# Where the split of the values' weights stands in layer 0 of a two-layer transformer kernel, and which engine makes its low parts

## The chip, the cores and the metric

The kernel runs on one core of one Trainium2 chip. The metric is the device time of one execution in microseconds (us). A core has five engines with instruction queues of their own: PE (TensorE, matrix products), DVE (VectorE), ACT (ScalarE), POOL (GpSimd) and SP (SyncE, which here only issues DMAs). Each engine works through its queue in the order in which it was built; engines wait for each other by semaphores.

## The reference

Two layers of a parallel-branch trunk are computed on 512 latent tokens and 256 context tokens of width 1024, in float32. Cut to what matters:

```python
hx = _rmsnorm(x, norm_g) * (1.0 + scale_x) + shift_x      # adaLN: scale and shift from c @ w_ada
px = hx @ w_in                                            # one projection, 5376 columns
a_k, a_v, b_k, b_v, a_q, b_q, a_z, b_z, g_a, g_b = _split(px, SPLIT_SIZES)
a_att = _na_latent(qa, ka, va, cka, cva, rpb, rows)       # neighbourhood attention, ka = rmsnorm(a_k)
b_att = _gqa_latent(qb, k_all, v_all)                     # grouped-query attention
out_x = _merge(a_att, b_att, a_z, b_z, g_a, g_b, w_o_a, w_o_b, w_out)
x_new = x + gate_x * out_x
```

The context tokens go through the same weights (in layer 0 all of them, in layer 1 only keys and values). The change concerns the first microseconds of layer 0: the norm and modulation of `x`, the first projection (`a_k`, the keys) and the second one (`a_v`, the values).

## The kernel before, in words

**Products in three parts.** A float32 operand is split into a high part (a cast to `fp32r`, made on ACT) and a low part (the difference of operand and high part, made on DVE or POOL). A product is then three matmuls (`mm3`, lines 351 to 353): high x high, high x low and low x high, all into one PSUM tile.

**Weights.** `load_w` (line 313) brings eight blocks of 128 x 512 of a weight matrix: a DMA on SP into a tile `raw` (three buffers in all), the cast `whi<-raw` on ACT (line 321), the low part `wlo<-raw,whi` (line 324) on the engine that `lo_eng(k)` names. `mix_lo` names VectorE for odd blocks and GpSimd for even ones. A `raw` buffer is free for the next DMA when its low part has been made. `whi` and `wlo` have eight buffers each, which the first projection's weights hold before the values' weights do.

**The start.** The first projection of layer 0 (the keys: six token tiles of 128, eight weight blocks, 144 matmuls) is woven into loads, norms, transposes and the adaLN modulation by `start_run` (line 1053). Its order is the string `START`, a list of tokens. The tokens that matter here carry the number of a channel block (0 to 7): `wh`/`wl` make the two parts of a weight block, `dot7.v` are four dot products on VectorE (line 1117, `jk<-wx,rawy`) that yield the modulation of block 7, `mf` turns sums into the two modulation columns (lines 208 and 209), `ts` applies them (line 1140 on ACT, 1142 on VectorE), `hi` and `lo` make the parts of the modulated activations (lines 1132 and 1134, `hx<-yT`), and `Pt.k` is token tile t times weight block k: three matmuls. After all tokens, `in_program_order` (line 392) ties each engine's instructions of the start to each other in the order of the string.

**What follows it.** `layer` (line 490) then evacuates the six PSUM tiles of the keys (copy to `y`, squares on ACT, sums on VectorE, the inverse root on POOL, lines 285 and 287), and calls `load_w` for the values' weights (line 620) and `tok_proj` for six token tiles (line 624): 24 matmuls each. The first of them writes PSUM tile `psf_818`, the second `psx_851`. Next come the weights of the queries (line 628). Everything outside the start is placed by the framework's scheduler: it works with a model of time and puts an instruction into an engine's queue where it expects it to be ready, if no tie forbids that. Nothing tied the eight casts and low parts of line 620 to the start, so that the scheduler was free to put them between the start's own instructions.

Of the kernel before, what the change touches and what calls it, by code (L numbers as in the profile page):

```python
# [22 lines left out]
KT = DM // 128  # L23
# [10 lines left out]
ON_PE, ON_DVE, ON_SP = mybir.EngineType.PE, mybir.EngineType.DVE, mybir.EngineType.SP  # L34
ON_ACT, ON_POOL = mybir.EngineType.Activation, mybir.EngineType.Pool
# [19 lines left out]
C_AK, C_AV, C_BKV, C_AQ, C_BQ, C_AZ, C_BZ, C_GA, C_GB = (  # L55
    0, 512, 1024, 1280, 1792, 2304, 2816, 3328, 4352)
# [6 lines left out]
def F(ap):  # L63
    return ap.bitcast(F32)
# [3 lines left out]
def hybrid_kernel(es: ExitStack, tc, x, ctx, cvec, w_ada, w_ada0, small, gvec, w_in, w_o_a, w_o_b, w_out,  # L68
                  bias_int, bias_edge, rope, ident_d, out):
    nc = tc.nc  # L70
    V, S, G, T = nc.vector, nc.scalar, nc.gpsimd, nc.tensor
# [10 lines left out]
    def nm(s):  # L82
        uid[0] += 1
        return f"{s}_{uid[0]}"

    def big(name):
        return bigp.tile([128, 3072], F32, tag="big", name=nm(name))
# [106 lines left out]
    def raw_tile():  # L194
        return wp.tile([128, 512], F32, tag="raw", name=nm("raw"), bufs=3)
# [117 lines left out]
    def load_w(src, col0, n, nk, lo_eng, k0=0, own=None, bufs=8):  # L313

        pool, x = (wp, "") if own is None else (own, "x")
        res = []
        for k in range(k0, k0 + nk):
            raw = raw_tile()
            nc.sync.dma_start(raw[:, :n], src[128 * k:128 * k + 128, col0:col0 + n])
            hi = pool.tile([128, 512], F32R, tag="whi" + x, name=nm("whi"), bufs=bufs)  # L320
            S.copy(hi[:, :n], raw[:, :n])  # L321
            lo = pool.tile([128, 512], F32R, tag="wlo" + x, name=nm("wlo"), bufs=bufs)
            e = lo_eng(k)
            e.tensor_tensor(lo[:, :n], raw[:, :n], F(hi[:, :n]), ALU.subtract)  # L324
            res.append((hi, lo))
        return res

    def load_w2(src, col0, nk, lo_eng):

        res = []  # L330
        for i in range(nk // 2):
            raw = raw_tile()
            nc.sync.dma_start(raw.rearrange("p (k n) -> p k n", k=2),
                              src[256 * i:256 * i + 256, col0:col0 + 256].rearrange("(k p) n -> p k n", k=2))
            hi = wp.tile([128, 512], F32R, tag="whi", name=nm("whi"), bufs=8)
            S.copy(hi, raw)  # L336
            lo = wp.tile([128, 512], F32R, tag="wlo", name=nm("wlo"), bufs=8)
            lo_eng(i).tensor_tensor(lo, raw, F(hi), ALU.subtract)  # L338
            res += [(hi[:, c:c + 256], lo[:, c:c + 256]) for c in (0, 256)]
        return res  # L340
# [3 lines left out]
    mix_lo = lambda k: V if k % 2 == 1 else G  # L344
# [44 lines left out]
                    mybir.DependencyClass.NoSync, mybir.DependencyReason.DATA), reason="program order")  # L389
                last = i.name  # L390

    def in_program_order(engines, seq):

        last = {}
        for i in seq:
            if i.engine in engines:
                if i.engine in last:
                    tc.add_manual_dep(i, last[i.engine], mybir.DependencyInfo(
                        mybir.DependencyClass.NoSync, mybir.DependencyReason.DATA), reason="program order")
                last[i.engine] = i.name  # L400

    def turn_late(n):

        while len(hp["late"]) > n:
            behind(ON_PE, hp["late"].pop(0))
# [84 lines left out]
    def layer(l, hx, nxt, mid):  # L490
        first = l == 0
# [4 lines left out]
        W = w_in[l]  # L496
# [114 lines left out]
        else:  # L611
            hp["p"] = bgp_es.enter_context(tc.tile_pool(name=f"cp{l}", bufs=1, reuse_waits="tile"))
            w = load_w(W, C_AK, 512, KT, mix_lo)
# [3 lines left out]
            run(bg, 1)  # L617
        per_bg = -(-len(bg) // (2 + qt))
        va = [big("va0"), big("va1")]
        w = load_w(W, C_AV, 512, KT, mix_lo)  # L620
        for t in range(6):
            if first:
                hp["lag"] = max(4 - t, 0)
# [4 lines left out]
        w = load_w(W, C_AQ, 512, KT, mix_lo, own=hp["p"])  # L628
# [18 lines left out]
        if True:  # L647
# [262 lines left out]
            w = load_w2(W, C_BKV, KT, mix_lo)  # L910
# [81 lines left out]
        with tc.tile_pool(name=f"mrg{l}", bufs=1, reuse_waits="tile") as mp:  # L992
# [37 lines left out]
            for n in range(2):  # L1030
                w = load_w(w_out[l], 512 * n, 512, KT, mix_lo)
# [21 lines left out]
    def start_run(wk, mm):  # L1053
# [91 lines left out]
        done, at = nc.cur_bb.bb.instructions, len(nc.cur_bb.bb.instructions)  # L1145
        for i in range(WARM):
            T.transpose(start_ps[5][:, 0:128], ident, ident)
        seq = list(done[at:])
        for tok in START.split():
            at = len(done)  # L1150
            if tok in setup:
                seq += done[setup[tok]]
            else:
                step(tok)
                seq += done[at:]
        in_program_order((ON_PE, ON_SP, ON_DVE, ON_ACT, ON_POOL), seq)

    start_w, start_ps, hx1 = {}, [], []

    def nxt():  # L1160
        if not hx1:
            hx1.extend([[big("hx") for _ in range(2)] for _ in range(2)])
        return hx1
    layer(0, hx0, nxt, start_run)
    layer(1, hx1, None, None)


# [69 lines left out]
```

## Time and profile before

| | |
|---|---|
| time, median of 3 runs | 1154.84 us (1154.14 to 1155.36) |
| the profiled execution | 1154.87 us |
| its span | 1152.3 us |
| mean granted TensorE clock | 0.998 |
| DMA | 135.08 MB, mean 117 GB/s |

The span runs from the first instruction to the last; 2.57 us of the execution lie around it. In the profile, rows of the timeline give the start in us from the span's start, the busy time in us, engine, line, operation and tiles; "x2" at a row's end means two instructions that were merged into it, and what stands in brackets is idle time before it with what ended it. PE rows are matmuls, which overlap: what counts is the distance from start to start. SPq rows are DMA issues.

### The profile page before, as it was taken

Reading aid. Unit: us, or ns where it says so; the run is one execution under the profiler, and the core shown is the slowest. Engines: PE = TensorE matmul, PEld = TensorE weight load, DVE = VectorE, ACT = ScalarE, POOL = GpSimd, SP = SyncE. Lnnn points to the kernel's source line nnn. Section 1 sums busy time; section 2 is a strip of 40 time slices with the busy share of each in tenths; the row PEclk is TensorE's granted clock in tenths of the full one; section 3 lists DMA queues with packets and bytes.
Section 4 is the critical chain, followed back from the end, with each engine's and each line's share of the span. In section 5 each row is a group of like instructions: output and inputs, shape, how many; then the busy total and the mean of one; then the engine's idle time right before and its main releaser. Section 6 shows DMA issues by size and latency. Waiting matters only on the chain.

```text
span 1152.3 us, 17437 instructions
## 1 busy us (share of the span) xinstructions
PE 1125.1 (98%) x6136; PEld 950.1 (82%) x6136; DVE 821.1 (71%) x1529; ACT 579.4 (50%) x1185; POOL 487.9 (42%) x453
## 2 busy tenths in 40 slices
PE   7899999999999999999999999999999999999998
PEld 5688888989988888878788787888888988887786
DVE  6866688997464687698588755569787665898563
ACT  6553266665433465566330365346666445766521
POOL 1172354454365243354411127245563664465321
PEclk9999999999999999999999999999999999999999
DMA  9734222233332332460343523533332333152133
GB/s 368 237 121 138 73 81 65 84 112 98 107 128 71 100 101 74 75 269 23 128 161 101 173 74 110 183 98 116 105 106 83 111 101 101 65 174 92 64 128 92
DMA packets 89694, 135.08 MB, mean 117 GB/s; under 512 B 10788, under 2 KB 52744, under 8 KB 88968
## 3 DMA queue, kind: packets, MB, share of 16 engines
q1 hardware_dynamic: 89328, 133.87, 36.6%
q8 instruction: 48, 0.79, 0.3%
q14 instruction: 38, 0.31, 0.1%
q10 hardware_dynamic: 280, 0.12, 0.0%
HBM read 116.63 MB, written 17.32 MB: 116 GB/s over the span
## 4 chain that ended last, share of the span: by engine, by line
PE 78%; DVE 8%; DMA 6%; issue 3%; ACT 3%; POOL 2%; SPq 0%; ACTq 0%; POOLq 0%; DVEq 0%
PE psx L353 12%; PE psx L351 11%; PE psx L352 11%; PE psf L351 9%; PE psf L353 9%; PE psf L352 9%; PE pst L666 4%; PE pss L715 2%; PE pss L716 2%; DMA raw<-in_w_in_dram 2%; PE psv L970 2%; PE pss L792 1%; PE pst L431 1%; PE psv L969 1%; DVE ptl L670 1%
## 5 line engine op out<-in xcount | busy, mean ns | idle before, releaser
L670 DVE TENSOR_TENSOR ptl<-pst,pth 128x512 fp32r<-128x512 f32 (+1 forms) x176 | 116.0, 672 | 46.7 <-ACT pth L669 45.6
L669 ACT CAST pth<-pst 128x512 fp32r<-128x512 f32 (+1 forms) x176 | 99.3, 577 | 87.3 <-PE pst L666 56.4
L338 POOL TENSOR_TENSOR wlo<-raw,whi 128x512 fp32r<-128x512 f32 x68 | 94.6, 1394 | 107.8 <-ACT whi L336 86.6
L351 PE MATMUL psx<-whi,hx 128*128 128x512 f32 (+1 forms) x368 | 138.3, 377 | 1.5 <-ACT hx L1132 1.5
L351 PE MATMUL psf<-hx,whi 128*128 128x512 f32 (+1 forms) x368 | 139.2, 378 | 0.0
L353 PE MATMUL psx<-whi,hx 128*128 128x512 f32 (+1 forms) x368 | 136.4, 371 | 2.1 <-DVE hx L1134 2.1
L352 PE MATMUL psf<-hx,whi 128*128 128x512 f32 (+1 forms) x368 | 138.1, 375 | 0.0
L353 PE MATMUL psf<-hx,wlo 128*128 128x512 f32 (+1 forms) x368 | 137.8, 374 | 0.0
L352 PE MATMUL psx<-wlo,hx 128*128 128x512 f32 (+1 forms) x368 | 135.9, 369 | 0.0
L324 POOL TENSOR_TENSOR wlo<-raw,whi 128x512 fp32r<-128x512 f32 x40 | 58.7, 1468 | 141.5 <-ACT whi L321 106.1
L336 ACT CAST whi<-raw 128x512 fp32r<-128x512 f32 x136 | 82.5, 622 | 50.8 <-DMA raw<-in_w_in_dram 32.5
L321 ACT CAST whi<-raw 128x512 fp32r<-128x512 f32 x88 | 54.0, 623 | 105.6 <-PE psx L353 41.8
L666 PE MATMUL pst<-ident,p 128*128 128x128 f32 x640 | 99.9, 272 | 1.4 <-DVE ptl L670 0.8
L666 PEld LDWEIGHTS pst<-ident,p 128*128 128x128 f32 x640 | 77.8, 140 | 13.0 <-DVE ptl L670 1.3
L338 DVE TENSOR_TENSOR wlo<-raw,whi 128x512 fp32r<-128x512 f32 x68 | 69.3, 1020 | 26.1 <-ACT whi L336 25.5
L655 POOL TENSOR_SCALAR r<-r 128x1 f32<-128x1 f32 x64 | 22.3, 349 | 151.7 <-DVE r L650 144.7
L656 POOL TENSOR_TENSOR p<-p,r 128x512 f32<-128x512 f32 (+1 forms) x64 | 83.9, 1310 | 5.1
L353 PEld LDWEIGHTS psx<-whi,hx 128*128 128x128 f32 x368 | 69.7, 189 | 14.6 <-DVE hx L1134 2.8
L351 PEld LDWEIGHTS psx<-whi,hx 128*128 128x128 f32 x368 | 69.7, 190 | 14.2 <-ACT hx L1132 2.3
L353 PEld LDWEIGHTS psf<-hx,wlo 128*128 128x128 f32 x368 | 69.4, 189 | 11.8
L352 PEld LDWEIGHTS psx<-wlo,hx 128*128 128x128 f32 x368 | 69.7, 189 | 10.8
L351 PEld LDWEIGHTS psf<-hx,whi 128*128 128x128 f32 x368 | 69.4, 188 | 10.8 <-ACT zt L516 0.2
(252 smaller groups left out, 3056.3 us busy)
## 6 DMA issues: line engine op xcount, KB each, us to landing
raw<-in_w_in_dram SPq DMA_DIRECT2D x168, 256.0 KB, 2.9
rawb<-in_w_ada_dram SPq DMA_DIRECT2D x64, 256.0 KB, 2.9
gs<-zt SPq DMA_DIRECT2D x32, 256.0 KB, 2.1
raw<-in_w_out_dram SPq DMA_DIRECT2D x32, 256.0 KB, 3.0
tg<-gs SPq DMA_DIRECT2D x4, 1536.0 KB, 7.4
rawx<-in_w_ada_dram SPq DMA_DIRECT2D x8, 512.0 KB, 7.7
raw<-in_w_o_a_dram SPq DMA_DIRECT2D x16, 256.0 KB, 2.7
raw<-in_w_o_b_dram SPq DMA_DIRECT2D x16, 256.0 KB, 2.8
```

The costliest lines, as they stand in the source:

```text
L321: S.copy(hi[:, :n], raw[:, :n])
L324: e.tensor_tensor(lo[:, :n], raw[:, :n], F(hi[:, :n]), ALU.subtract)
L336: S.copy(hi, raw)
L338: lo_eng(i).tensor_tensor(lo, raw, F(hi), ALU.subtract)
L351: T.matmul(ps, lhs[0], rhs[0], start=first, stop=False)
L352: T.matmul(ps, lhs[0], rhs[1], start=False, stop=False)
L353: T.matmul(ps, lhs[1], rhs[0], start=False, stop=last)
L656: G.tensor_tensor(p[:, c0:c1], p[:, c0:c1], r[:, i:i + 1].to_broadcast([128, c1 - c0]), ALU.mult)
L666: T.transpose(pt[:, c0:c0 + 128], src, ident)
L669: S.copy(hi[:, n0:n1], pt[:, n0:n1])
L670: V.tensor_tensor(lo[:, n0:n1], pt[:, n0:n1], F(hi[:, n0:n1]), ALU.subtract)
L715: T.matmul(ps[:, c0:c0 + n], q, sl(kh), start=True, stop=False)
```

## The change

The casts and low parts of the values' weights in layer 0 get a tie: in the program's order, their instructions on VectorE and ScalarE follow the last instruction that the start has on that engine. For that, `in_program_order` takes and returns the table of each engine's last instruction, and the start leaves it in `start_last`. The DMAs of these weights are not tied. Also, in layer 0 all eight low parts of these weights are made on VectorE, where blocks 0, 2, 4 and 6 were made on GpSimd. Layer 1 keeps `mix_lo` and has no tie. All else in the program's text stays; as the scheduler places what is not tied, the order of other instructions can follow.

```diff
-    def in_program_order(engines, seq):
+    def in_program_order(engines, seq, last):
 
-        last = {}
         for i in seq:
             if i.engine in engines:
                 if i.engine in last:
                     tc.add_manual_dep(i, last[i.engine], mybir.DependencyInfo(
                         mybir.DependencyClass.NoSync, mybir.DependencyReason.DATA), reason="program order")
                 last[i.engine] = i.name
+        return last
...
-        w = load_w(W, C_AV, 512, KT, mix_lo)
+        at = len(nc.cur_bb.bb.instructions)
+        w = load_w(W, C_AV, 512, KT, (lambda k: V) if first else mix_lo)
+        if first:
+            in_program_order((ON_DVE, ON_ACT), nc.cur_bb.bb.instructions[at:], start_last)
...
-        in_program_order((ON_PE, ON_SP, ON_DVE, ON_ACT, ON_POOL), seq)
+        start_last.update(in_program_order((ON_PE, ON_SP, ON_DVE, ON_ACT, ON_POOL), seq, {}))
 
-    start_w, start_ps, hx1 = {}, [], []
+    start_w, start_ps, start_last, hx1 = {}, [], {}, []
```

The order of the built program shows two places of it. The first is VectorE at the end of the start, from the reduction of `mf6` (line 1121; 1124 in the changed kernel, whose lines below the edit stand three further down) to the first evacuation of the keys. `wlo` rows of line 324 are low parts of the values' weights, rows that write `jk` are the dot products, and `hx_102` is the low part of the activations. Before:

```order
L1121 TENSOR_REDUCE sums_613<-pst_604 128x4
L324 TENSOR_TENSOR wlo_780<-raw_776,whi_778 128x512
L208 TENSOR_SCALAR modc<-sums_613,bsc,g_128 128x2
L209 TENSOR_SCALAR modc<-sums_613,gcol 128x2
...
L324 TENSOR_TENSOR wlo_792<-raw_788,whi_790 128x512
L1134 TENSOR_TENSOR hx_102<-yT_104,hx_100 128x768
L208 TENSOR_SCALAR modc<-sums_594,bsc,g_128 128x2
L209 TENSOR_SCALAR modc<-sums_594,gcol 128x2
L324 TENSOR_TENSOR wlo_804<-raw_800,whi_802 128x512
L1134 TENSOR_TENSOR hx_102<-yT_104,hx_100 128x768
L453 COPY y_707<-psx_135 128x512
```

And the same place on VectorE in the changed kernel:

```order
L1124 TENSOR_REDUCE sums_613<-pst_604 128x4
L208 TENSOR_SCALAR modc<-sums_613,bsc,g_128 128x2
L209 TENSOR_SCALAR modc<-sums_613,gcol 128x2
...
L1137 TENSOR_TENSOR hx_102<-yT_104,hx_100 128x768
L208 TENSOR_SCALAR modc<-sums_594,bsc,g_128 128x2
L209 TENSOR_SCALAR modc<-sums_594,gcol 128x2
L1137 TENSOR_TENSOR hx_102<-yT_104,hx_100 128x768
L324 TENSOR_TENSOR wlo_774<-raw_770,whi_772 128x512
L324 TENSOR_TENSOR wlo_780<-raw_776,whi_778 128x512
L324 TENSOR_TENSOR wlo_786<-raw_782,whi_784 128x512
L453 COPY y_707<-psx_135 128x512
```

Three low parts (of blocks 1, 3 and 5) stood between the start's instructions and now stand behind its last one, with those of blocks 0 and 2 from GpSimd's queue.

The second place is TensorE where the values' projection begins, behind the last three matmuls of the keys (`psx_138`). `whi_772`, `whi_778`, `whi_784` and `whi_790` are blocks 0 to 3. From the changed kernel:

```order
L353 MATMUL psx_138<-whi_570,hx_102 128x512
L351 MATMUL psf_818<-whi_772,hx_99 128x512
...
L353 MATMUL psf_818<-whi_784,hx_101 128x512
L351 MATMUL psf_818<-whi_790,hx_99 128x512
L351 MATMUL psx_851<-whi_772,hx_99 128x512
L352 MATMUL psx_851<-wlo_774,hx_99 128x512
L353 MATMUL psx_851<-whi_772,hx_101 128x512
L351 MATMUL psx_851<-whi_778,hx_99 128x512
L352 MATMUL psx_851<-wlo_780,hx_99 128x512
L353 MATMUL psx_851<-whi_778,hx_101 128x512
L352 MATMUL psf_818<-wlo_792,hx_99 128x512
```

Before, the first token tile went through seven blocks before the second one began; now six matmuls of the second tile stand between the first and the second matmul of block 3, because the scheduler expects block 3's low part later than before. TensorE's queue up to the end of the keys is the same in both.

## The prediction

> **What bounds the kernel now.** The page's engine line comes first:
>
> ```profile
> PE 1125.1 (98%) x6136; PEld 950.1 (82%) x6136; DVE 821.1 (71%) x1529; ACT 579.4 (50%) x1185; POOL 487.9 (42%) x453
> ```
>
> TensorE is busy for 98% of the span: time is won only where it stands or runs slowly. So the next view is who TensorE waited for:
>
> ```profile
> PE psx L353 <- DVE hx L1134: 2.1, 1, 2.1
> PE psv L970 <- DVE ptl L670: 2.0, 3, 1.5
> PE psx L351 <- ACT hx L1132: 1.5, 1, 1.5
> ```
>
> Behind the first load, the longest single waits are for `hx`, the activations' parts that the start makes. The table by stage (span, then busy time of PE, PEld, DVE, ACT, POOL, then granted clock) shows what stands around them:
>
> ```profile
> 45.00:49.50 4.50, 4.50 (x22) 3.65 (x20) 4.50 (x7) 0.62 (x2) 3.34 (x2) 1.00 0.38 117
> 49.50:51.33 1.83, 0.33 (x3) 0.00 (x1) 1.83 (x5) 1.39 (x3) 0.00 (x0) 1.00 0.51 143
> 51.33:55.40 4.07, 1.99 (x7) 1.34 (x8) 3.09 (x6) 1.41 (x3) 1.40 (x1) 1.00 0.39 103
> 55.40:58.78 3.38, 3.38 (x10) 2.60 (x9) 1.65 (x2) 1.60 (x3) 0.00 (x0) 0.51 0.89 288
> 58.78:62.00 3.22, 3.22 (x15) 2.66 (x14) 0.22 (x1) 1.60 (x3) 0.41 (x1) 0.99 0.36 138
> 1000.00:1100.00 100.00, 96.97 (x502) 78.45 (x501) 82.69 (x124) 61.84 (x116) 48.31 (x42) 1.00 0.30 101
> ```
>
> From 49.50 to 55.40 TensorE stands for over half the time, VectorE is nearly always busy, and then for 3.38 us the clock is 0.51. TensorE's own rows there:
>
> ```profile
> 46.04 0.39 PE L353 MATMUL psx<-whi,hx 128*128 128x512 f32 x1
> ...
> 49.44 0.39 PE L353 MATMUL psx<-whi,hx 128*128 128x512 f32 x1
> 51.33 0.50 PE L351 MATMUL psx<-whi,hx 128*128 128x512 f32 x1 [1.50 <-ACT hx L1132]
> 51.66 0.40 PE L352 MATMUL psx<-wlo,hx 128*128 128x512 f32 x1
> 54.14 0.50 PE L353 MATMUL psx<-whi,hx 128*128 128x512 f32 x1 [2.08 <-DVE hx L1134]
> ...
> 58.78 0.43 PE L351 MATMUL psx<-whi,hx 128*128 128x512 f32 x1
> ...
> 64.30 0.39 PE L351 MATMUL psf<-whi,hx 128*128 128x512 f32 x1
> ```
>
> From 46.04 to 49.44 lie 15 distances: 0.227 us per matmul undisturbed; I use 0.228. The row at 51.33 is the first matmul of `P5.6`, which needs `hi6`; the row at 54.14 its third, which needs `lo6`; 58.78 is `P5.7`; 64.30 is the first matmul of the values.
>
> What held `hx` back is on VectorE, and beside it on POOL:
>
> ```profile
> 37.35 0.17 DVE L1121 TENSOR_REDUCE sums<-pst 128x4 f32<-128x16 f32 x1 [0.18 <-PE pst L1110]
> 37.56 0.29 DVE L208 TENSOR_SCALAR modc<-sums,bsc,g 128x2 f32<-128x2 f32 x1
> 37.76 0.22 DVE L209 TENSOR_SCALAR modc<-sums,gcol 128x2 f32<-128x2 f32 x1
> ...
> 45.42 0.17 DVE L1121 TENSOR_REDUCE sums<-pst 128x4 f32<-128x16 f32 x1
> 45.50 1.69 DVE L324 TENSOR_TENSOR wlo<-raw,whi 128x512 fp32r<-128x512 f32 x1
> 47.11 1.25 DVE L208 TENSOR_SCALAR modc<-sums,bsc,g 128x2 f32<-128x2 f32 x1
> 48.27 0.22 DVE L209 TENSOR_SCALAR modc<-sums,gcol 128x2 f32<-128x2 f32 x1
> 48.41 1.21 DVE L1117 CUSTOM_DVE_ANT_0 jk<-wx,rawy 128x1024 bf16<-128x1024 f32 x1
> ...
> 49.55 0.86 DVE L1142 TENSOR_SCALAR yT<-yT,modc 128x512 f32<-128x512 f32 x2
> 50.33 1.21 DVE L1117 CUSTOM_DVE_ANT_0 jk<-wx,rawy 128x1024 bf16<-128x1024 f32 x1
> ...
> 51.47 0.68 DVE L324 TENSOR_TENSOR wlo<-raw,whi 128x512 fp32r<-128x512 f32 x1
> 52.08 2.01 DVE L1134 TENSOR_TENSOR hx<-yT,hx 128x768 fp32r<-128x768 f32 x1
> 54.01 0.28 DVE L208 TENSOR_SCALAR modc<-sums,bsc,g 128x2 f32<-128x2 f32 x1
> 54.20 0.22 DVE L209 TENSOR_SCALAR modc<-sums,gcol 128x2 f32<-128x2 f32 x1
> ...
> 57.04 0.96 DVE L1134 TENSOR_TENSOR hx<-yT,hx 128x768 fp32r<-128x768 f32 x1
> ```
>
> ```profile
> 44.31 4.03 POOL L324 TENSOR_TENSOR wlo<-raw,whi 128x512 fp32r<-128x512 f32 x2 [20.32 <-ACT whi L321]
> 51.87 1.40 POOL L324 TENSOR_TENSOR wlo<-raw,whi 128x512 fp32r<-128x512 f32 x1 [3.54 <-ACT whi L321]
> ```
>
> Two low parts of the values' weights stand in front of `mf6` and of `lo6`. Beside POOL's low parts VectorE's instructions stretch: line 324 takes 1.69 instead of 0.68 us, line 208 1.25 instead of 0.29, `lo6` 2.01 instead of the 0.96 of `lo7`.
>
> **The change part by part: the start.** Without rows of line 324 on VectorE, and with POOL's gone from there, I set VectorE's rows together anew from 45.42, with undisturbed distances: 0.21 to line 208, 0.20 to line 209, 0.13 (48.27 to 48.41 is 0.14) to the dot product at 45.96, 1.14 to `ts6` at 47.10, 0.78 to the last dot product at 47.88, 1.14 to `lo6` at 49.02, done at 49.98. For `hi6` and `ts7` ACT's rows give the lengths:
>
> ```profile
> 50.44 0.83 ACT L1132 CAST hx<-yT 128x768 fp32r<-128x768 f32 x1 [0.44 <-DVE yT L1142]
> ...
> 54.46 1.31 ACT L1140 ACTIVATE yT<-yT,modc 128x512 f32<-128x512 f32 x2 [2.66 <-DVE modc L209]
> 55.67 0.60 ACT L321 CAST whi<-raw 128x512 fp32r<-128x512 f32 x1
> 56.18 0.83 ACT L1132 CAST hx<-yT 128x768 fp32r<-128x768 f32 x1
> ```
>
> `ts6` ends at 47.96, `hi6` at 48.82. TensorE would reach `P5.6` at 49.44 + 0.228 = 49.67 and needs `lo6` two matmuls later, at 50.12: the first wait goes, the second goes with some 0.1 us to spare (54.09 to 54.14: 0.05 pass between the end of `lo6` and its reader). A row of VectorE begins 0.08 before the last one ends (54.01 against 54.09), so `mf7` begins at 49.90 and ends, as at 54.01 to 54.42, at 50.3; `ts7` runs from 50.36, `hi7` starts 1.21 later and ends at 52.40, `lo7` at 53.38. `P5.7` stands 15 matmuls behind `P5.6`, at 53.09, and needs `lo7` at 53.55: again 0.1 us to spare. What is late next is therefore this same chain; I allow 0.1 us for it, and 0.6 as its bad end (0.3 at each of the two places).
>
> From 49.44 to 64.30 are 14.86 us and 40 distances (39 matmuls of 13 groups, and the first of the values); 40 x 0.228 = 9.12. The difference, **5.74 us**, is what the start can win, and it has three parts: 1.66 (51.33 less 49.67), 2.25 (54.14 less 51.89), and the rest, 1.83, at the 0.51 clock and the first matmuls behind a wait. The clock part alone is 3.38 x 0.49 = 1.66, by the stage row.
>
> That this last part goes with the waits is an inference. For it: the slow stretch begins 1.3 us behind the second wait, and of the stages above only the one behind two long waits is slow. Against it: the 1.5 us wait of line 970 lies between 1000 and 1100, where the clock stayed at 1.00. [...] I follow the rows, a low clock right behind the only place with two long waits within 5 us, and keep the other as a rival.
>
> **The values' weights.** They are what the change puts at risk. ACT casts blocks 0 to 2 behind `hi7`, at 0.6 us each from 52.4 to 54.3; VectorE makes their low parts behind `lo7`, at 0.68 us each, done at 54.1, 54.7 and 55.4. The values now begin at 58.56 instead of 64.30: blocks 0 to 2 are ready 3 us before. Blocks 3 to 7 wait for a `raw` buffer, so each DMA starts only when the low part three blocks earlier is done. The answer for line 319 gives the flight:
>
> ```profile
> DMA to landing us min/median/max: 2.6/2.7/9.8
> ```
>
> Block 3: issued 54.1, landed 56.8, cast 57.4, low part 58.1. TensorE wants its cast behind nine matmuls, at 60.6, and its low part behind six more, at 62.2: 3.2 and 4.1 us to spare. Block 6 is next on that buffer: issued 58.1, landed 60.8, cast by 61.6 and low part by 62.9, as each stands behind one or two evacuations of the keys (an estimate: 0.6 to 0.7 us apiece). Its cast is wanted behind 30 matmuls and four transposes, at 65.8. No wait. On VectorE four low parts more are 4 x 0.68 = 2.7 us, in a place where it was idle for 3.0 of 3.22 us (row 58.78 to 62.00); TensorE wants the keys' evacuations only in the transposes between the values' matmuls, the first of them 30 matmuls in, at 65.4. POOL loses four low parts and is free sooner for its inverse roots. On SP the two loads of `cb` and two of `rawb` for later dot products now stand before block 3's; they wait only for matmuls from before 30 us, land in the ten us before block 3's is due, and cost nothing; were they late by a flight, it would be 2.7 of the 3.2 us to spare.
>
> **Later.** Between 60 and 150 us TensorE shows no wait; queues from there to the merge of layer 0 are the same, so the shift passes on whole. In the merge and layer 1 a few instructions swap places. I take 0, and 1 us either way as bounds.
>
> Sum: 1154.87 - 5.74 + 0.1 = **1149.2 us** (its span 1146.7). The profiled execution lies 0.03 from the median, so it stands for it. Own range: 1148.2 (nothing lost, 0.9 won later) to 1150.2.
>
> **The rivals.** A measurement of this kernel can tell 0.2%, 2.3 us, from no change.
>
> *The slow clock stays* (10%): 1149.2 + 1.66 = 1150.9. For it: the gaps are short and one of 1.5 us elsewhere had no such effect. Against: of the other stages above, none with TensorE busy throughout is slow.
>
> *Given back later* (13%): the swapped instructions, or evacuations that now meet the values' matmuls sooner, bring 1 to 3.3 us of new waits: 1150.2 to 1152.5. For it: TensorE's listed waits for `ptl`, up to 1.5, depend on close races. Against: the order of almost all queues is kept.
>
> *The values' weights come late: slower* (4%). If flights took L instead of 2.7, block 6, which hangs on two flights in a row, would be late from 2 x (L - 2.7) = 4.2, L = 4.8. At L = 7 block 3's wait (1.1) and its own (3.1) come to 4.2 us, and with a second slow clock (1.66) eat 5.74: that is where it turns slower. At the longest flight seen, 9.8, the waits are 3.9 and 5.9, so 1149.2 + 9.8 + 1.7 = 1160.7. Against: 2.7 is the median, and the 9.8 lies in the start's dense loads.
>
> *No effect* (3%): 1154.9, if something else that I don't see paces `hx`. The order of VectorE speaks against it.
>
> The forecast keeps 70%. The range 1148.0 to 1151.3 holds it, the slow clock, and a third of "given back": 84%. Faster by over 2.3 us: 70 + 10 + 12 = 92%, of which I keep 0.9; same 0.06; slower 0.04.
>
> **What would show it.** Right: no wait of TensorE for `hx` over 0.3 us between 45 and 60, clock 1.00 there, the first values' matmul near 58.6, line 324 at about 0.68 on VectorE, `lo6` near 0.96. Wrong: a wait for `whi` or `wlo` at line 351 or 352 between 58 and 70 (the weights), a clock near 0.5 after 50 (the rival's 1.66), or a first values' matmul near 58.6 with a span that shrank by less than 4.5 (given back).

## The result and the profile after

The changed kernel took 1148.99 us (median of 4 runs, 1148.41 to 1149.14), the kernel before in the same job 1155.1 us (4 runs, 1154.14 to 1156.52): the ratio is 0.9945, 95% interval 0.9928 to 0.9962. The profiled execution of after took 1149.07 us.

The page of after opens with its span and the engines' busy time:

```profile
span 1147.0 us, 17434 instructions
...
PE 1123.5 (98%) x6136; PEld 949.2 (83%) x6136; DVE 818.3 (71%) x1533; ACT 580.3 (51%) x1185; POOL 483.0 (42%) x449
```

The span is 5.3 us shorter; another 0.5 us is missing around it (2.07 us instead of 2.57). Asked who TensorE waited for between 20 and 150 us, the trace of after lists nobody; before it listed the two waits for `hx`. The stages (span, busy time of PE, PEld, DVE, ACT, POOL, then granted clock), in the stretches that the prediction used:

```profile
49.50:51.33 1.83, 1.83 (x9) 1.42 (x8) 0.88 (x3) 0.91 (x2) 0.00 (x0) 1.00 0.00 0
51.33:55.40 4.07, 4.07 (x19) 3.15 (x18) 2.77 (x4) 3.33 (x6) 0.00 (x0) 1.00 0.06 7
55.40:58.78 3.38, 3.38 (x17) 2.79 (x16) 2.50 (x4) 2.55 (x6) 1.09 (x2) 1.00 0.69 229
```

TensorE is busy through all three, and where 0.51 stood the clock is 1.00. VectorE in the timeline of after, from the reduction of `mf6` on:

```profile
45.50 0.17 DVE L1124 TENSOR_REDUCE sums<-pst 128x4 f32<-128x16 f32 x1
45.71 0.29 DVE L208 TENSOR_SCALAR modc<-sums,bsc,g 128x2 f32<-128x2 f32 x1
...
47.96 1.22 DVE L1120 CUSTOM_DVE_ANT_0 jk<-wx,rawy 128x1024 bf16<-128x1024 f32 x1
...
49.10 0.95 DVE L1137 TENSOR_TENSOR hx<-yT,hx 128x768 fp32r<-128x768 f32 x1
49.97 0.28 DVE L208 TENSOR_SCALAR modc<-sums,bsc,g 128x2 f32<-128x2 f32 x1
50.16 0.22 DVE L209 TENSOR_SCALAR modc<-sums,gcol 128x2 f32<-128x2 f32 x1
52.62 0.96 DVE L1137 TENSOR_TENSOR hx<-yT,hx 128x768 fp32r<-128x768 f32 x1 [2.24 <-ACT hx L1135]
53.50 1.89 DVE L324 TENSOR_TENSOR wlo<-raw,whi 128x512 fp32r<-128x512 f32 x3
```

`lo6` (49.10) starts 3.60 us behind the reduction, not 6.66; it takes 0.95 instead of 2.01 us, line 208 behind the reduction 0.29 instead of 1.25. The three low parts come behind `lo7` (52.62), in 1.89 us together. TensorE's rows, `P5.6` with its third matmul, `P5.7` with its third and the one behind it, and the first of the values:

```profile
49.74 0.39 PE L351 MATMUL psx<-whi,hx 128*128 128x512 f32 x1
...
50.19 0.41 PE L353 MATMUL psx<-whi,hx 128*128 128x512 f32 x1
...
53.19 0.39 PE L351 MATMUL psx<-whi,hx 128*128 128x512 f32 x1
...
53.64 0.50 PE L353 MATMUL psx<-whi,hx 128*128 128x512 f32 x1
53.97 0.39 PE L351 MATMUL psf<-whi,hx 128*128 128x512 f32 x1
...
58.76 0.39 PE L351 MATMUL psf<-whi,hx 128*128 128x512 f32 x1
```

The values start 5.54 us sooner (64.30 to 58.76). From there to the end of the span are 1088.24 us, before 1088.0: 0.24 us is given back. The one wait of TensorE that is new in the later part lies between 900 and 1000 us; a wait of 0.4 for `whi`, between 500 and 800 us, is gone:

```profile
PE psf L351 <- ACT zt L516: 0.6, 1, 0.6
```

### The profile page after: what moved, and what is told of

Same layout as the page of the kernel before. It is cut to its first block, busy times and chain, and to the rows that moved or that the text cites. A ratio compares the mean times of both kernels' runs of the same rounds, so it can differ in the third digit from the quotient of the medians.

```text
span 1147.0 us, 17434 instructions
## 1 busy us (share of the span) xinstructions
PE 1123.5 (98%) x6136; PEld 949.2 (83%) x6136; DVE 818.3 (71%) x1533; ACT 580.3 (51%) x1185; POOL 483.0 (42%) x449
## 4 chain that ended last, share of the span: by engine, by line
PE 80%; DVE 7%; DMA 4%; issue 3%; ACT 3%; POOL 2%; SPq 0%; POOLq 0%; ACTq 0%; DVEq 0%
PE psx L353 12%; PE psx L352 12%; PE psx L351 11%; PE psf L351 9%; PE psf L352 9%; PE psf L353 9%; PE pst L669 4%; DMA raw<-in_w_in_dram 2%; PE pss L718 2%; PE pss L719 2%; PE psv L973 2%; PE psv L972 1%; PE pss L795 1%; PE pst L431 1%; DMA rawb<-in_w_ada_dram 1%
## 5 line engine op out<-in xcount | busy, mean ns | idle before, releaser
L338 POOL TENSOR_TENSOR wlo<-raw,whi 128x512 fp32r<-128x512 f32 x68 | 95.6, 1409 | 105.1 <-ACT whi L336 83.9
L324 POOL TENSOR_TENSOR wlo<-raw,whi 128x512 fp32r<-128x512 f32 x36 | 50.9, 1416 | 110.0 <-ACT whi L321 74.6
```

## The experiments

The theory: low parts of line 324 ahead of the start's instructions on VectorE, and GpSimd's beside them, held `hx` back; the two waits that followed also lowered the clock. The rivals: only one half of the edit matters; the slow stretch has another cause; the weights are close to being late. One measure runs through what follows. It is the distance from the third matmul of `P5.6`, the reader of `lo6`, to the first matmul of the values: 37 distances of the same work in every kernel, all behind the waits at `P5.6`.

### The tie alone

The change, with the low parts shared out as before:

```diff
-        w = load_w(W, C_AV, 512, KT, (lambda k: V) if first else mix_lo)
+        w = load_w(W, C_AV, 512, KT, mix_lo)
```

> The tie alone: low parts of blocks 0, 2, 4, 6 stay on GpSimd. Theory (what stood ahead of lo6 and lo7 in VectorE's queue, and GpSimd beside it, made the waits): nearly all of the gain stays, 1149.3 to 1150.0 us; the 0.3 to 1.0 us lost against the change is lo7, which now runs beside GpSimd's first low part (0.96 stretched towards 2.0), seen as a wait of TensorE for hx near 53.6. Rival (the choice of VectorE brings half of the gain): about 1152, with TensorE waiting for wlo from GpSimd behind 58 us.

Measured: 1149.09 us (5 runs, 1148.67 to 1149.74), ratio to before 0.9953 (0.9941 to 0.9964): the change's own time within the spread of either. The loss that was expected at `lo7` did not come. VectorE and then GpSimd there:

```profile
52.73 0.96 DVE L1137 TENSOR_TENSOR hx<-yT,hx 128x768 fp32r<-128x768 f32 x1 [2.24 <-ACT hx L1135]
53.77 1.61 DVE L324 TENSOR_TENSOR wlo<-raw,whi 128x512 fp32r<-128x512 f32 x1
```

```profile
53.30 3.24 POOL L324 TENSOR_TENSOR wlo<-raw,whi 128x512 fp32r<-128x512 f32 x2 [29.48 <-ACT whi L321]
```

`lo7` had started when GpSimd's low part began at 53.30, and kept 0.96 us; the next instruction of VectorE, at 53.77, took 1.61 instead of 0.68. So the stretch is there again, in a place where nobody waits for it. The tie does the work.

### The engine alone

The kernel before, with all eight low parts on VectorE and no tie:

```diff
-        w = load_w(W, C_AV, 512, KT, mix_lo)
+        w = load_w(W, C_AV, 512, KT, (lambda k: V) if first else mix_lo)
```

> VectorE alone, without the tie. The scheduler now puts five low parts ahead of lo6 on VectorE (two ahead of mf6, one ahead of ts6, two ahead of lo6). Theory: GpSimd's stretch goes (3.0 us on VectorE's rows before), queueing grows from two to five low parts (3 x 0.61 us more). Set together from 45.5: hi6 ends at about 51.1, lo6 at 52.9, two waits of TensorE of 1.5 and 1.3 us; the values' first matmul at 61.4 with the clock at 1.00, at 63.1 with a slow stretch. Time 1152.0 to 1153.7. Rival (only the place in the queue counts, GpSimd's neighbourhood nothing): three more low parts, slower than before, about 1157.

Measured: 1153.75 us (11 runs, 1152.17 to 1154.53), ratio 0.999 (0.9981 to 0.9998). TensorE's waits between 20 and 150 us, then VectorE:

```profile
PE psx L351 <- ACT hx L1132: 1.4, 1, 1.4
PE psx L353 <- DVE hx L1134: 0.9, 1, 0.9
PE pst L431 <- DVE y L419: 0.6, 1, 0.6
```

```profile
45.70 1.28 DVE L324 TENSOR_TENSOR wlo<-raw,whi 128x512 fp32r<-128x512 f32 x2
46.91 0.28 DVE L208 TENSOR_SCALAR modc<-sums,bsc,g 128x2 f32<-128x2 f32 x1
...
52.10 0.95 DVE L1134 TENSOR_TENSOR hx<-yT,hx 128x768 fp32r<-128x768 f32 x1
```

Without GpSimd beside it none of these rows stretches: 0.28 instead of 1.25, 0.95 instead of 2.01, a low part 0.64. But five low parts stand ahead of `lo6`, so the wait for `hi6` stays and the second one falls only to 0.9. So the stretching beside GpSimd accounts for part of the waits (2.08 against 0.93 us for `lo6`); moving it away without the tie puts three more low parts in the same way, and wins 0.1%.

### The tie on VectorE only, and the low parts on GpSimd

Two more versions of the tie. In the first, ScalarE's casts are free again, and those of blocks 0 to 2 go back ahead of `hi6`; in the second, `pool_lo` names GpSimd for every block:

```diff
-            in_program_order((ON_DVE, ON_ACT), nc.cur_bb.bb.instructions[at:], start_last)
+            in_program_order((ON_DVE,), nc.cur_bb.bb.instructions[at:], start_last)
```

```diff
-        w = load_w(W, C_AV, 512, KT, (lambda k: V) if first else mix_lo)
+        w = load_w(W, C_AV, 512, KT, pool_lo if first else mix_lo)
```

> The change with the tie on VectorE alone: the casts of blocks 0 to 2 may stand ahead of hi6 on ScalarE again, the low parts may not. Theory (the low parts made the waits, the casts none, since ScalarE had 0.4 us and more of idle time ahead of hi6): as the change, 1148.5 to 1149.5. Rival (the casts ahead of hi6 hold it back, 0.62 us each): up to 0.6 us more wait at P5.6, about 1149.6 to 1150.2.

> The tie, with all eight low parts of the values' weights on GpSimd. Theory (the weights had 3 to 4 us to spare, and the order on TensorE follows what the scheduler expects): lo7 stretched as with the tie alone, 0.3 to 1.0 us, and 0 to 2 us of waits for wlo behind 58 us: 1149.3 to 1152. Rival (the weights are close to late as soon as they are tied): waits for wlo of 4 us and more, 1153 or over, with a slow clock behind them.

Measured: 1148.47 us (5 runs, 1148.36 to 1149.92; ratio 0.9947, 0.9934 to 0.9961) and 1148.92 us (5 runs, 1148.46 to 1149.37; ratio 0.9947, 0.9935 to 0.996). Both stand with the change, the second below the 1149.3 that was the least expected. In the first, the last two of ScalarE's casts of blocks 0 to 2 stand from 43.85 to 45.10, 2.49 us of idle time ahead of `hi6`. So they cost nothing there, and with the low parts behind the start their engine made no difference in the time (1148.99 us on VectorE, 1149.09 shared out, 1148.92 on GpSimd). Even GpSimd, at 4.05 us for three of them, is early enough; its row, and beside it `lo7` on VectorE, which again began first and kept 0.96:

```profile
52.81 4.05 POOL L324 TENSOR_TENSOR wlo<-raw,whi 128x512 fp32r<-128x512 f32 x3 [28.98 <-ACT whi L321]
```

```profile
52.24 0.96 DVE L1137 TENSOR_TENSOR hx<-yT,hx 128x768 fp32r<-128x768 f32 x1 [2.24 <-ACT hx L1135]
```

### Every block loaded twice

The change, with the DMA of each of the eight blocks issued twice in a row into the same buffer (`times` is 2 for the values' weights of layer 0 and 1 elsewhere):

```diff
-            nc.sync.dma_start(raw[:, :n], src[128 * k:128 * k + 128, col0:col0 + n])
+            for _ in range(times):
+                nc.sync.dma_start(raw[:, :n], src[128 * k:128 * k + 128, col0:col0 + n])
```

> The change with each block of the values' weights loaded twice into the same buffer, one DMA after the other, which makes the flight about 5.4 instead of 2.7 us. By the prediction's working (block 3 to spare 3.2 us, block 6 behind two flights late from 4.8): block 6 late by 2 x 2.7 - 4.2 = 1.2 us if TensorE's order were kept; the scheduler mixes three token tiles now, which hides more. Theory: 0 to 1.2 us more than the change, 1149.0 to 1150.2. Rival (weights near their limit): 3 us more or worse, 1152 and over.

Measured: 1149.48 us (5 runs, 1148.67 to 1150.72), ratio 0.9954 (0.9941 to 0.9966), and again no wait of TensorE from 20 to 110 us. The casts of the blocks on ScalarE (line 322 there), the row at 60.20 being block 3:

```profile
51.60 1.66 ACT L322 CAST whi<-raw 128x512 fp32r<-128x512 f32 x3
60.20 0.62 ACT L322 CAST whi<-raw 128x512 fp32r<-128x512 f32 x1 [1.81 <-DMA raw<-in_w_in_dram]
61.73 0.61 ACT L322 CAST whi<-raw 128x512 fp32r<-128x512 f32 x1
62.78 0.61 ACT L322 CAST whi<-raw 128x512 fp32r<-128x512 f32 x1
```

Block 3's cast starts 3.4 us later than in after (56.80), and nobody waited for it: the scheduler, which knows of the second load, put other matmuls first (the first one of block 3 starts at 63.29, in after at 60.80). In a kernel placed for it, then, even a doubled flight is not late. The change's own order on TensorE is not tested by it: nine matmuls behind this run's first of the values (58.30), that order would want the cast at 60.34, and it ends at 60.82, so an estimate is 0.5 us late.

### The waits filled with transposes

The kernel before, with 12 transposes of the identity ahead of `P5.6` (the token `F0.12`) and 16 between its second and third matmul, into a PSUM tile that nobody reads. `hx` comes as late as before, but TensorE has something to do meanwhile:

```diff
         T.matmul(ps, lhs[0], rhs[0], start=first, stop=False)
         T.matmul(ps, lhs[0], rhs[1], start=False, stop=False)
+        if fz is not None:
+            for i in range(16):
+                T.transpose(fz, ident, ident)
         T.matmul(ps, lhs[1], rhs[0], start=False, stop=last)
```

> The kernel before with its two waits for hx, but 12 transposes of the identity matrix into a spare PSUM tile in TensorE's queue ahead of P5.6 and 16 between its second and third matmul, so that TensorE works while it would wait (about 1.3 of 1.7 and 1.8 of 2.2 us). Theory (the slow clock comes from TensorE's idleness in the waits): the waits stay as long, the clock stays at 1.00, the slow stretch of 3.38 us goes: 1.5 to 1.7 us less than before, about 1153.4. Rival (the slow stretch has another cause): clock 0.51 stays behind 55, time as before, 1155.

Measured: 1154.65 us (12 runs, 1153.43 to 1158.99), ratio 1.0005 (0.9995 to 1.0016): in the time, nothing; some 1.5 us had been expected. In the profile, the stage and TensorE's rows at `P5.6` (line 356 is the third matmul of each product there):

```profile
55.40:58.78 3.38, 3.38 (x16) 2.62 (x15) 1.46 (x2) 2.38 (x4) 0.00 (x0) 1.00 0.89 259
```

```profile
52.55 1.91 PE L355 MATMUL pst<-ident 128*128 128x128 f32 x16
54.81 0.49 PE L356 MATMUL psx<-whi,hx 128*128 128x512 f32 x1 [0.35 <-DVE hx L1141]
...
63.46 0.39 PE L351 MATMUL psf<-whi,hx 128*128 128x512 f32 x1
```

The slow stretch is missing: 54.81 to 63.46 are 8.65 us, where before 54.14 to 64.30 are 10.16. One profile alone does not show that the transposes did it, as two profiles with unfilled waits, further down, lack the stretch too. The mean clocks of the executions say more: every profile here without the slow stretch has a mean clock of 0.999 or 1.0, every one with it 0.997 or 0.998, and 0.999 or more was granted in 9 of 12 executions with filled waits, but in 2 of 38 of the kernel before. In this execution the gain passed on: the reduction of `mf6` came 0.65 later (46.07), and the span is 0.8 us shorter, as 1.51 less 0.65 says. Over twelve executions the median does not show it; some took up to 1158.99 us, for a reason that the one profile doesn't hold. The run speaks for TensorE's idleness as the cause of the low clock; of the time it shows nothing.

### One wait put back

The change, with the last dot product ahead of `lo6` made three times:

```diff
-P3.3 dot7.1 P1.3 ts6.0.6v P5.3 P3.4 dot7.0 hi6.0.6 P4.5 P3.5 lo6.0.6v P2.4 mf7 P5.6 ts7.0.6s P0.5
+P3.3 dot7.1 P1.3 ts6.0.6v P5.3 P3.4 dot7.0 dot7.0 dot7.0 hi6.0.6 P4.5 P3.5 lo6.0.6v P2.4 mf7 P5.6 ts7.0.6s P0.5
```

> The changed kernel with the last dot product of block 7 made three times on VectorE (the same sums), which holds lo6 back by 2.28 us. One wait of TensorE of about 2.2 us near 50.1, none ahead of it. Theory (a low clock needs about two such waits within 5 us): the clock stays at 1.00, 2.2 us more than the change, about 1151.2. Rival (one wait of this length is enough): a slow stretch behind it, 3.9 us more, about 1152.9.

Measured: 1153.27 us (11 runs, 1152.62 to 1154.88), ratio 0.9986 (0.9977 to 0.9995), near the number that a falling clock gave. But the profile shows one wait of 2.1 us, the clock at 1.00 behind it, and other waits later instead, one of them in the wait list of the whole run:

```profile
PE psx L352 <- POOL wlo L324: 0.9, 1, 0.9
```

The median fits one theory, the trace the other. So the same kernel was profiled once more, together with three others whose stretch behind the waits was in doubt.

### Four more profiles: does the clock follow the waits?

Nothing is edited: the kernel before twice more, the kernel with one wait put back, and the one with the low parts on VectorE.

> The kernel before, unchanged, profiled a second time. If the low clock comes from the two waits of TensorE for hx (2.1 and 1.5 us), it falls again within some 3 us behind the second wait, to about 0.5 for some 3 us, and nowhere else between 60 and 150 us; the distance from lo6's reader to the first matmul of P5.7 is 4.6 us again instead of 3.2. If the low stretch of the first profile had another cause, it lies elsewhere or is missing, and that distance is 3.2 us.

> The kernel before, unchanged, profiled a third time: as for the second look. If the low clock needs the waits but not every execution with waits has it, one of the looks may be without it and is then about 1.5 us shorter from lo6's reader to the first values' matmul.

> The kernel with one wait of 2.1 us, profiled a second time. Its first profile showed the clock at 1.00 throughout, its other executions a mean clock between 0.997 and 1.0. If one wait can bring the low clock in some executions, this look may show a stage near 0.5 behind the wait and a first values' matmul near 62.5 instead of 60.9; if only two waits can, it is 1.00 again.

> The kernel before with all low parts on VectorE and no tie (waits of 1.4 and 0.9 us), profiled a second time. First profile: clock 1.00 throughout, first values' matmul at 61.76. If two shorter waits can bring the low clock too, a stage near 0.5 stands behind them and the first values' matmul comes some 1.5 us later; if not, the rows repeat.

They took 1155.73, 1155.11, 1153.06 and 1154.19 us, one execution each. The stages of one microsecond or two in the second profile with one wait put back:

```profile
51.00:53.00 2.00, 0.39 (x1) 0.39 (x2) 1.89 (x5) 0.08 (x1) 0.00 (x0) 0.82 0.00 0
53.00:54.00 1.00, 1.00 (x3) 0.77 (x3) 0.00 (x0) 1.00 (x2) 0.00 (x0) 0.50 0.00 0
54.00:55.00 1.00, 1.00 (x4) 0.74 (x3) 0.00 (x0) 0.97 (x3) 0.00 (x0) 0.50 0.00 0
55.00:56.00 1.00, 1.00 (x5) 0.78 (x4) 0.87 (x1) 1.00 (x3) 0.00 (x0) 0.65 0.00 0
56.00:57.00 1.00, 1.00 (x6) 0.84 (x5) 1.00 (x3) 0.66 (x2) 0.00 (x0) 1.00 0.00 0
```

And TensorE's rows there, where the distance of two matmuls is 0.43 us and, from 55.75 on, 0.23:

```profile
49.94 0.39 PE L352 MATMUL psx<-wlo,hx 128*128 128x512 f32 x1
52.61 0.79 PE L353 MATMUL psx<-whi,hx 128*128 128x512 f32 x1 [2.28 <-DVE hx L1137]
53.20 0.63 PE L351 MATMUL psf<-whi,hx 128*128 128x512 f32 x1
53.63 0.63 PE L352 MATMUL psf<-wlo,hx 128*128 128x512 f32 x1
...
55.75 0.39 PE L351 MATMUL psx<-whi,hx 128*128 128x512 f32 x1
55.98 0.39 PE L352 MATMUL psx<-wlo,hx 128*128 128x512 f32 x1
...
62.55 0.39 PE L351 MATMUL psf<-whi,hx 128*128 128x512 f32 x1
```

Here one wait of 2.28 us, in a kernel that had none, brought the clock to 0.50 for 3.4 us (0.18 x 2 + 0.50 + 0.50 + 0.35 = 1.71 us of clock lost, at half speed 3.42 us). The waits and what follows them, in the profiles read for it (lost clock is summed as here, from stages of one or two microseconds):

| profile | waits of TensorE at `P5.6`, us | clock lost, us | reader of `lo6` to the values, us |
|---|---|---|---|
| before, first | 1.50, 2.08 | 1.71 | 54.14 to 64.30: 10.16 |
| before, second | 1.39, 2.08 | 1.71 | 55.28 to 65.34: 10.06 |
| before, third | 1.25, 2.09 | 1.70 | 54.19 to 64.09: 9.90 |
| one wait put back, second | 2.28 | 1.71 | 52.61 to 62.55: 9.94 |
| VectorE only, second | 1.44, 0.64 | 1.70 | 52.83 to 62.96: 10.13 |
| VectorE only, first | 1.44, 0.93 | 0 | 53.11 to 61.76: 8.65 |
| one wait put back, first | 2.13 | 0 | 52.22 to 60.91: 8.69 |
| waits filled | 0.19, 0.35 | 0 | 54.81 to 63.46: 8.65 |
| after | none | 0 | 50.19 to 58.76: 8.57 |
| the tie alone | none | 0 | 50.29 to 58.85: 8.56 |

In these profiles the low clock comes with the waits: its start moves with them from 52.3 to 55.4 us, in the five profiles without them the clock column shows 1.00 in every stage from 45 to 100 us (in after also in every stage of 10 us from 0 to 1140), and it costs 1.4 us (the mean of the five rows with it, 10.04, less 8.62, the mean of the five rows without it). It needed neither two waits (one of 2.28 us brought it) nor GpSimd (1.44 and 0.64 us brought it with all low parts on VectorE). But it did not come in every execution: the same two kernels showed it in one profile and not in another. The mean clock of each execution says the same more coarsely: before, 0.996 to 0.999 in 38 executions; the five kernels without waits, 0.999 to 1.0 in 24; the two kernels with waits that were profiled twice, 0.997 to 1.0. The two executions of before at 0.999 took 1153.25 and 1153.34 us, the shortest of the 38 (median 1154.9): 1.6 us less, in the time itself.

Its size in the total time of the kernel with one wait is not settled. Its six executions at 0.999 or more took 1153.5 us on average, its five below that 1153.3; with VectorE only, 1153.1 (seven) and 1154.0 (four). The first profile, without the slow stretch, ended at a span of 1152.0 us, the second, with it, at 1150.9: from the values' start to the end are 1091.09 us in the first and 1088.35 in the second. A wait for `wlo` of 0.9 us (0.3 in the second) and waits of 0.6 and 0.5 us in transposes stand in the first alone; what brings such later waits was not tried.

## Why the prediction held, point by point

**What held `hx` back: shown.** The tie removes both waits with any engine making the low parts (four versions, 1148.47 to 1149.09 us); the engine without the tie leaves 2.3 us of waits and wins 0.1%. That the low parts on VectorE and GpSimd's beside it act together was right, too: without GpSimd the second wait was 0.93 and 0.64 in the two profiles, instead of 2.08.

**The chain set together anew: right to 0.2 us.** `lo6` ended at 50.05 (predicted 49.98), its reader started at 50.19 (needed by 50.12). `P5.7` came at 53.19 (53.09), `lo7` ended at 53.58 (53.38). The 0.1 us allowed for this chain is there, at `lo7`: its reader stands 0.45 behind `P5.7`'s first matmul, as usual, but the next one 0.33 behind it instead of 0.23. Of the differences, 0.08 is the whole start: the reduction came at 45.50 instead of 45.42.

**The gain at the start: 5.54 against 5.74 less 0.1.** The 0.1 us missing is the later start, and rounding.

**The third part, 1.83 us at the low clock: the inference held, and its size was near.** The rival in which the slow clock stays is excluded by the table. The low clock costs 1.4 us by it, and 1.6 us in the profile that the prediction used. There, nine distances from 55.41 on take 3.64 us where nine of 0.228 are 2.05:

```profile
54.48 0.39 PE L351 MATMUL psf<-whi,hx 128*128 128x512 f32 x1
...
55.41 0.59 PE L352 MATMUL psx<-wlo,hx 128*128 128x512 f32 x1
...
59.05 0.39 PE L352 MATMUL psx<-wlo,hx 128*128 128x512 f32 x1
```

The rest of the 1.83 is the first matmul behind each wait, 0.1 us apiece (51.33 to 51.66, 54.14 to 54.48). Two points of the argument were wrong. That the slow stretch begins 1.3 us behind the second wait holds for that profile only: by the stages, it begins at 55.1, 53.8 and 52.3 us in three of the others, where the wait ends at 55.28, 54.19 and 52.61. And it took two long waits within 5 us as the condition: one of 2.28 us did it, while two of 1.44 and 0.93 did not.

That the gaps are short, which the rival had for it, did not keep the clock up: the profile's row at 52.61 is a wait of 2.28 us with half the clock behind it. Each of the five slow stretches is 3.4 us long (1.70 or 1.71 us lost at a clock of 0.50), and in two of the three kernels that showed it, it came in one profile and not in the other. The length of the waits does not separate these profiles: together they are 2.08 to 3.58 us in the five rows of the table with the low clock, and 2.13 and 2.37 us in the two rows of unfilled waits without it. What decides in which executions it comes was not shown.

**The weights: right.** ScalarE's casts of blocks 3 and 4 in after, and TensorE's matmul that wants the first of them:

```profile
56.80 1.36 ACT L321 CAST whi<-raw 128x512 fp32r<-128x512 f32 x2 [0.68 <-DMA raw<-in_w_in_dram]
```

```profile
60.80 0.39 PE L351 MATMUL psf<-whi,hx 128*128 128x512 f32 x1
```

Block 3 landed at 56.80 as predicted and had over 3 us to spare; every block loaded twice cost no wait either, in a kernel whose TensorE order was placed for it. One sum of the rival with late weights is off: by the working's own 4.2 us to spare, block 6's own wait is 3.3 us at L = 7 and 6.1 at 9.8, not 3.1 and 5.9, so that its worst case is 1160.9.

**Later: 0.24 us given back,** within the 1 us allowed; 0.6 us of new waiting for `zt` is the row that shows it, partly made up by the 0.4 for `whi` that is gone.

**The time around the span: not foreseen.** The sum ended at a span of 1146.7 and took 2.57 us around it for granted. The span came out at 1147.0, and 2.07 around it: the two errors, 0.3 up and 0.5 down, partly cancel in the 1149.07 us, so that the sum came within 0.2 us is in part luck. In the median of the executions, 2.5 us lie around the span for before and for the kernel with the filled waits, and 1.9 to 2.1 us for the other versions. Some 0.4 us of the measured gain are therefore not TensorE's waits. No profile shows what lies there, and its cause stays open.

## What to carry to other kernels

Where a chain is ordered by hand and the rest is left to a scheduler, look in the built order for foreign instructions between the chain's own on each engine it uses; tying them behind its last instruction was worth more here (1149.09 us with the tie alone, 1154.91 before) than choosing a better engine for them, which left them in the way (1153.75). A wait's price on TensorE was not its length alone (1.4 us more where the low clock followed): measure from the waited-for matmul to a fixed later one, and compare that distance with an undisturbed profile. One profile of a kernel with waits may miss the low clock or show it (five of the seven profiles with unfilled waits at `P5.6` showed it), so take a second before building on it.

## What the hardware showed that was not expected

- The low clock: 0.50 for 3.4 us each time, after one wait of 2.28 us or two of 1.44 and 0.64; absent in another execution after one of 2.13, or two of 1.44 and 0.93.
- At the very start, the clock column does not show what the distances do: behind TensorE's first 4.87 us without work, 12 transposes of the identity take 2.82 us in before; the 12 in the first filled wait take 1.47. The column says 1.00 beside both.
- VectorE beside GpSimd: low parts and line 208 of VectorE that started while GpSimd made a low part stretched (0.68 to 1.61 in the kernel with the tie alone, 0.68 to 1.69 and 0.29 to 1.25 in before), an instruction that had started before it did not (`lo7`, 0.96 with GpSimd's low part starting 0.57 us into it, both times). Not every instruction stretched: beside GpSimd's low parts the reduction at 45.42 in before kept its 0.17 us, and in the tied kernel with the low parts on GpSimd the copy of line 453 at 55.87 and the reduction of line 415 at 56.47 took 0.69 and 0.67, as in after (0.69, 0.68).
- The time around the span differs between versions of one kernel by 0.4 us, steadily (before 2.2 to 2.65 us over 38 executions; after 2.02 to 2.14 over 4).
